# The last norm of a layer taken out of the end and put under the last expert

## The chip, the cores and the metric

The kernel runs on one core of one Trainium2 chip. The metric is the time of one execution on the device in microseconds (us). Engines are named as in the profile: PE (TensorE), DVE (VectorE), ACT (ScalarE), POOL (GpSimd), SP (SyncE); each runs its own instructions in the order in which the kernel writes them down.

## The reference, cut to what matters

One transformer layer: attention and an mLSTM side by side, a norm, a mixture of 16 experts in which each expert picks its 128 tokens of the 1024, and a last norm:

```python
x_new = _layer_norm(ALPHA * x + g1 * mix, ln1_g, ln1_b)
moe = _expert_choice_ffn(x_new * (1 + sc2) + sh2, ...)      # 16 experts, 128 tokens each
x_new = _layer_norm(ALPHA * x_new + g2 * moe, ln2_g, ln2_b) # the norm that is moved
# expert: ((silu(xe @ wg) * (xe @ wu)) @ wd) * g_e, added to the rows idx_e
```

Rows are 1024 wide, an expert's hidden width is 2816. A token can be picked by several experts or by none.

## The kernel before

Only the expert stage and the end matter here. `ACC` is a 1024x1024 table in device memory that holds `ALPHA * x_new`; each expert adds its gated 128 rows to it.

The experts run as 96 steps (`steps`, six for each expert; the last expert is steps 90 to 95; step 95 is half as wide). For each step the weights come as tiles of 1 MB (`we_st`, read by SP into 8 buffers), are split by ACT into a rounded part (`weH`, L1362) and by DVE into the rest (`weL`, L1371). PE multiplies three products for each pair. The loop of L1654 writes down for each `i`, in this order:

- PE: gate product of step i (`ps_gu`), transpose of `hh` of step i-1 (`ps_hT`, L1621); ACT and DVE: `hTH` and `hTL` of step i-1 (L1624, L1625);
- ACT and DVE: the two gate tiles of step i+1; then the piece `extra[2 * i]`, if there is one;
- PE: up product of step i; ACT and DVE: the two up tiles of step i+1;
- PE: down product of step i-1 (`ps_y`, L1635). After an expert's last one DVE gates it into `yo` (L1641) and POOL scatters it with an adding indirect DMA into `ACC` (L1688);
- ACT and DVE: `hh` of step i (L1613, L1614), the two down tiles of step i; then the piece `extra[2 * i + 1]`.

`extra` holds small pieces of work at fixed places; before, only the top-k of the first experts used it. `weH` and `weL` have six buffers each, so a tile is split at most about one step ahead of PE.

The end (`load_z`, `finish`): the two rows of norm weights (`lnv2`) and the 1024 rows of `ACC` are read during step 95 (`zt`, L1650). The last expert's rows are not scattered: after its down product DVE gates them (L1641), ACT and DVE split them (L1798, L1799), and PE adds them to each of eight blocks of 128 rows through a 0/1 matrix (`sel`, L1809, L1810). For each block DVE adds and sums (L1811), ACT squares (L1814) and takes the root, DVE scales by the weights (L1816), ACT by the root (L1821), POOL adds the bias (L1822), and SP writes `out_y` (L1823; the last two blocks in halves by DVE, L1827, L1829).

Of the kernel before, what the change touches and what calls it, by code (L numbers as in the profile page):

```python
# [8 lines left out]
F32 = mybir.dt.float32  # L9
F32R = mybir.dt.float32r  # L10
BF16 = mybir.dt.bfloat16
# [150 lines left out]
def f32(ap):  # L162
    return ap.bitcast(F32)


class K:
# [1151 lines left out]
    def phase_tail(self, nexp=NE, final=True):  # L1318
# [309 lines left out]
        def down(i, h, py):  # L1628
            e, s = steps[i]
            n = 4 if s < 5 else 2  # L1630
            for k in range(n):
                H, L = conv[i, "d", k // 2]
                for m, (a, b) in enumerate(((h[0], H), (h[0], L), (h[1], H))):
                    for j in range(2):
                        nc.tensor.matmul(py[j], a[:, k, :], b[:, k % 2, 512 * j:512 * j + 512],  # L1635
                                         start=(s == 0 and k == 0 and m == 0), stop=(s == 5 and k == n - 1 and m == 2))

        def gated(py, g, out):
            for j in range(2):
                cs = slice(512 * j, 512 * j + 512)  # L1640
                nc.vector.scalar_tensor_tensor(out[:, cs], py[j], g, g2[:, cs], op0=ALU.mult, op1=ALU.mult)  # L1641

        zs = []

        def load_z(n):
            if not zs:
                self.lnv2 = [self.brow(rp, f"ln2{j}", d["lnv"][2 + j:3 + j, :], tag=f"R{j}") for j in range(2)]
            while len(zs) < n:
                zt = self.stage.tile([128, 2, D], F32, name="zt", tag="st")
                nc.sync.dma_start(zt, self.ACC[256 * len(zs):256 * len(zs) + 256].rearrange("(a p) c -> p a c", p=128))  # L1650
                zs.append(zt)

        extra = self.topk_pieces(R)
        for i in range(N + 1):  # L1654
            if i < N:
# [4 lines left out]
            if i > 0:  # L1660
                hT = trans(i - 1, hh)
                if i < N and s == (5 if e == 1 else 4) and e + 1 < nexp:
                    info[e + 1] = self.index_of(e + 1, oh, mx, final and e + 2 == nexp)
                if i + 1 < N:
                    conv_to(end[i + 1, "g"])
                if final and i == N - 1:
                    load_z(3)
                if 2 * i in extra:
                    extra[2 * i]()
# [9 lines left out]
            if i > 0:  # L1679
                ep, sp = steps[i - 1]  # L1680
                if sp == 0:
                    py = [self.pY.tile([128, 512], F32, name="ps_y", tag="y") for _ in range(2)]
                down(i - 1, hT, py)
                if sp == 5 and not (final and i == N):
                    idx, g = info[ep][:2]
                    yo = rp.tile([128, D], F32, name="yo", tag="yo")
                    gated(py, g, yo)
                    nc.gpsimd.indirect_dma_start(out=self.ACC, in_=yo, in_offset=None, compute_op=ALU.add,  # L1688
                                                 out_offset=bass.IndirectOffsetOnAxis(ap=idx[:, :1], axis=0))
            if i < N:  # L1690
                hh = act_mul(i, pg, pu)
# [5 lines left out]
        if final:  # L1697
            load_z(4)
            self.finish(gated, py, info[nexp - 1], zs, mx, mA)
        es.close()  # L1700
# [44 lines left out]

    def index_of(self, e, oh, mx, last=False):
        nc, rp = self.nc, self.rp
# [15 lines left out]
        nc.gpsimd.tensor_add(g, ax[:, 5:6], ax[:, 4:5])  # L1763
        if last:
            nc.gpsimd.tensor_scalar(ax[:, 6:7], ax[:, 0:1], 128.0, ax[:, 1:2], op0=ALU.mult, op1=ALU.add)
            nc.gpsimd.tensor_scalar(ax[:, 8:16], self.tid[:, 1:9], -128.0, ax[:, 6:7], op0=ALU.mult, op1=ALU.add)
        return idx, g, xe, ax
# [14 lines left out]

    def finish(self, gated, py, info, zs, mx, pool):

        nc, d, rp = self.nc, self.d, self.rp
        idx, g, xe, ax = info
        lg, lb = self.lnv2
        sel = mx.tile([128, 8, 128], F32R, name="sel", tag="xe")
        for c in range(8):
            nc.vector.tensor_scalar(sel[:, c, :], self.slots, ax[:, 8 + c:9 + c], None, op0=ALU.is_equal)  # L1790
        yo = rp.tile([128, D], F32, name="yo", tag="yo")
        yH = mx.tile([128, D], F32R, name="yH", tag="xeH")
        yL = mx.tile([128, D], F32R, name="yL", tag="xeL")
        gated(py, g, yo)
        nc.scalar.activation(rp.tile([128, 1], F32, name="tiny"), self.eps, AF.Sqrt)
        for i in range(2):
            cs = slice(512 * i, 512 * i + 512)
            nc.scalar.copy(yH[:, cs], yo[:, cs])  # L1798
            nc.vector.tensor_sub(yL[:, cs], yo[:, cs], f32(yH[:, cs]))  # L1799
        s = rp.tile([128, 8, 8], F32, name="fst")  # L1800
        junk = rp.tile([128, D], BF16, name="junk", tag="oh")
        zt = [zs[t // 2][:, t % 2, :] for t in range(8)]
        wt = [pool.tile([128, D], F32, name="fw", tag=("weH", "weL")[t % 2]) for t in range(8)]

        def add(t):
            for i in range(2):
                cs = slice(512 * i, 512 * i + 512)
                ps = self.pG.tile([128, 512], F32, name="ps_z", tag="g")
                nc.tensor.matmul(ps, sel[:, t, :], yH[:, cs], start=True, stop=False)  # L1809
                nc.tensor.matmul(ps, sel[:, t, :], yL[:, cs], start=False, stop=True)  # L1810
                nc.vector.scalar_tensor_tensor(zt[t][:, cs], ps, 1.0, zt[t][:, cs], op0=ALU.mult, op1=ALU.add,  # L1811
                                               accum_out=s[:, t, i:i + 1])
            nc.vector.tensor_scalar(s[:, t, 2:3], s[:, t, 0:1], s[:, t, 1:2], -1.0 / D, op0=ALU.add, op1=ALU.mult)
            nc.scalar.activation(junk, zt[t], AF.Square, bias=s[:, t, 2:3], accum_out=s[:, t, 3:4])  # L1814
            nc.scalar.activation(s[:, t, 4:5], s[:, t, 3:4], AF.Sqrt, scale=1.0 / D, bias=self.eps)
            nc.vector.scalar_tensor_tensor(wt[t], zt[t], s[:, t, 2:3], lg, op0=ALU.add, op1=ALU.mult)  # L1816

        def scale(t):
            nc.vector.reciprocal(s[:, t, 4:5], s[:, t, 4:5])
            if t < 6:  # L1820
                nc.scalar.activation(wt[t], wt[t], AF.Copy, scale=s[:, t, 4:5])  # L1821
                nc.gpsimd.tensor_add(wt[t], wt[t], lb)  # L1822
                nc.sync.dma_start(self.o["y"][128 * t:128 * t + 128], wt[t])  # L1823
                return
            for i in range(2):
                cs = slice(512 * i, 512 * i + 512)
                nc.vector.scalar_tensor_tensor(wt[t][:, cs], wt[t][:, cs], s[:, t, 4:5], lb[:, cs], op0=ALU.mult,  # L1827
                                               op1=ALU.add)
                nc.sync.dma_start(self.o["y"][128 * t:128 * t + 128, cs], wt[t][:, cs])  # L1829

        for t in range(8):
            add(t)
            if t:
                scale(t - 1)
        scale(7)


# [29 lines left out]
```

## Time and profile before

| | us |
|---|---|
| median of 3 runs (lowest to highest) | 2413.16 (2404.59 to 2416.39) |
| profiled execution | 2414.1 |
| its span in the trace | 2412.3 |
| PE busy in the span | 2253.0 (93%) |
| DVE busy | 1986.7 (82%) |
| ACT busy | 1443.7 (60%) |
| POOL busy | 553.4 (23%) |

The span runs from the first to the last instruction. "Busy" is an average over the whole span; the expert stage takes about its last two thirds, the end about 43 us. A row of the timeline gives the start, the time from the first start to the last end of a run of like instructions, engine, line and operation; in brackets stands how long the engine was idle before it and what ended that.

### The profile page before, as it was taken

The page shows a single profiled execution, that of the slowest core. Times are in us where ns is not written, and L with a number is a line of the kernel's source. Part 1 is how long each engine was busy: PE and PEld are TensorE (multiplying, and loading weights), DVE is VectorE, ACT ScalarE, POOL GpSimd, SP SyncE. Part 2 cuts the span into 40 slices and gives each one's busy share as a digit, 9 for nine tenths or more (in the row PEclk, how much of TensorE's full clock was granted, in tenths as well). Part 3 has the DMA queues.
Part 4 walks back from the last instruction along what each step waited for, and adds up shares of the span by engine and source line. Part 5 has one row for each costly group of instructions (what it writes and reads, how often), then busy time and mean ns, then how long its engine had stood idle before and what let it go on. Part 6 is the DMA issues. An engine that isn't in the chain of part 4 may idle for free.

```text
span 2412.3 us, 33490 instructions
## 1 busy us (share of the span) xinstructions
PE 2253.0 (93%) x12606; PEld 1934.8 (80%) x12606; DVE 1986.7 (82%) x2379; ACT 1443.7 (60%) x1573; POOL 553.4 (23%) x495
## 2 busy tenths in 40 slices
PE   8978999888999599799999999999999999999994
PEld 7878988778888477588888888888888888888883
DVE  7756587757765699988988989889889889889897
ACT  2333433346754466466776777767767767767774
POOL 3424455414444345520000010000000100100102
PEclk9999999999999699899999999999999999999997
DMA  7576447489967598889999999999999999999992
GB/s 287 202 258 221 132 142 221 145 257 297 278 193 244 201 326 316 305 287 394 373 372 398 371 378 390 372 381 383 371 394 377 369 394 376 372 398 371 380 390 99
DMA packets 357971, 748.93 MB, mean 310 GB/s; under 512 B 17073, under 2 KB 106609, under 8 KB 356145
## 3 DMA queue, kind: packets, MB, share of 16 engines
q1 hardware_dynamic: 345344, 703.99, 80.7%
q0 software_dynamic: 12320, 42.28, 5.9%
q8 instruction: 99, 1.62, 0.3%
q14 instruction: 64, 0.52, 0.1%
q10 hardware_dynamic: 144, 0.52, 0.1%
HBM read 690.35 MB, written 63.72 MB: 313 GB/s over the span
## 4 chain that ended last, share of the span: by engine, by line
PE 69%; DVE 15%; DMA 8%; issue 4%; ACT 3%; SPq 1%; POOL 0%; DVEq 0%; ACTq 0%; POOLq 0%
PE ps_gu L1606 36%; PE ps_y L1635 18%; DVE weL L1371 3%; PE ps_o L1408 3%; DMA wr<-in_w_ada 2%; DMA abi<-in_bias 2%; PE ps_in L438 2%; PE ps_hT L1621 1%; PE ps_o L1145 1%; DVE y L546 1%; ACT weH L1362 1%; DVE wr L643 1%; PE ps_in L325 1%; PE ps_xe L1777 1%; DVE m L1722 1%
## 5 line engine op out<-in xcount | busy, mean ns | idle before, releaser
L1371 DVE TENSOR_TENSOR weL<-we_st,weH 128x2048 fp32r<-128x2048 f32 x512 | 1172.7, 2337 | 84.7 <-ACT weH L1362 84.7
L1362 ACT CAST weH<-we_st 128x2048 fp32r<-128x2048 f32 x528 | 982.4, 1915 | 55.7 <-PE ps_y L1635 38.7
L1606 PE MATMUL ps_gu<-weH,xeH 128*128 128x512 f32 (+1 forms) x1536 | 582.5, 379 | 0.0
L1606 PE MATMUL ps_gu<-weL,xeH 128*128 128x512 f32 (+1 forms) x1536 | 573.6, 373 | 1.0 <-DVE weL L1371 1.0
L1606 PE MATMUL ps_gu<-weH,xeL 128*128 128x512 f32 (+1 forms) x1536 | 573.8, 374 | 0.0
L1606 PEld LDWEIGHTS ps_gu<-weH,xeL 128*128 128x128 f32 x1536 | 290.7, 189 | 51.9 <-DVE xeL L1780 0.3
L1606 PEld LDWEIGHTS ps_gu<-weL,xeH 128*128 128x128 f32 x1536 | 291.4, 190 | 50.4 <-DVE weL L1371 1.4
L1606 PEld LDWEIGHTS ps_gu<-weH,xeH 128*128 128x128 f32 x1536 | 291.1, 190 | 48.9 <-ACT xeH L1779 0.2
L1624 ACT CAST hTH<-ps_hT 128x512 fp32r<-128x512 f32 x96 | 52.9, 552 | 411.2 <-PE ps_hT L1621 411.2
L1635 PE MATMUL ps_y<-weH,hTH 128*128 128x512 f32 x704 | 219.3, 393 | 0.5 <-ACT hTH L1624 0.5
L1635 PE MATMUL ps_y<-weH,hTL 128*128 128x512 f32 x704 | 217.7, 391 | 0.5 <-DVE hTL L1625 0.3
L1635 PE MATMUL ps_y<-weL,hTH 128*128 128x512 f32 x704 | 217.8, 391 | 0.0
L1759 POOL TENSOR_SCALAR idx<-ax 128x1 int32<-128x1 f32 x15 | 6.6, 442 | 668.4 <-ACT ax L1752 668.4
L1635 PEld LDWEIGHTS ps_y<-weH,hTL 128*128 128x128 f32 x704 | 132.5, 188 | 29.2 <-DVE hTL L1625 1.3
L1635 PEld LDWEIGHTS ps_y<-weL,hTH 128*128 128x128 f32 x704 | 132.7, 189 | 27.9
L1635 PEld LDWEIGHTS ps_y<-weH,hTH 128*128 128x128 f32 x704 | 131.5, 189 | 27.1 <-ACT hTH L1624 0.7
L438 PE MATMUL ps_in<-wH,uH 128*128 128x256 f32 (+1 forms) x448 | 134.1, 299 | 12.6 <-DVE ev L485 8.7
L1688 POOL DMA_INDIRECT ACC<-yo,idx x15 | 24.2, 1614 | 487.0 <-DVE yo L1641 487.0
L438 PE MATMUL ps_in<-wL,uH 128*128 128x256 f32 (+1 forms) x448 | 131.3, 293 | 0.0
L438 PE MATMUL ps_in<-wH,uL 128*128 128x256 f32 (+1 forms) x448 | 131.1, 293 | 0.0
L1371 POOL TENSOR_TENSOR weL<-we_st,weH 128x2048 fp32r<-128x2048 f32 x16 | 97.4, 6090 | 113.5 <-ACT weH L1362 109.6
L1625 DVE TENSOR_TENSOR hTL<-ps_hT,hTH 128x512 fp32r<-128x512 f32 x96 | 61.6, 642 | 70.1 <-ACT hTH L1624 70.1
(396 smaller groups left out, 3817.0 us busy)
## 6 DMA issues: line engine op xcount, KB each, us to landing
we_st<-in_wg SPq DMA_DIRECT2D x176, 1024.0 KB, 10.0
we_st<-in_wu SPq DMA_DIRECT2D x176, 1024.0 KB, 10.1
we_st<-in_wd SPq DMA_DIRECT2D x176, 1024.0 KB, 9.7
wr<-in_w_ada SPq DMA_DIRECT2D x32, 512.0 KB, 4.4
ws<-in_w_in POOLq DMA_DIRECT2D x36, 256.0 KB, 3.7
abi<-in_bias SPq DMA_DIRECT2D x16, 480.0 KB, 7.3
wa<-in_w_ada SPq DMA_DIRECT2D x7, 1024.0 KB, 7.5
avr<-AVC SPq DMA_DIRECT2D x32, 192.0 KB, 4.6
```

What stands on the lines that cost most here:

```text
L325: nc.tensor.matmul(ps[:, :w], a[:, k, ms], b[:, k, t0:t0 + w], start=(k == 0 and i == 0), stop=(k == 7 and i == 2))
L438: nc.tensor.matmul(ps[:, :w], l, r, start=(k == 0 and i == 0), stop=(k == 7 and i == 2))
L546: nc.vector.scalar_tensor_tensor(y[:, o:o + w], x[:, i0 + j:i0 + j + w], cw[:, j:j + 1], y[:, o:o + w], op0=ALU.mult, op1=ALU.add)
L643: nc.vector.tensor_tensor_reduce(w, w, scr, 1.0, 0.0, ALU.mult, ALU.add, self.ada_r[:, n:n + 1])
L1362: nc.scalar.copy(H, staged[pos[2]])
L1371: (eng or (nc.gpsimd if pool else nc.vector)).tensor_sub(L, staged.pop(pos[1]), f32(H))
L1408: nc.tensor.matmul(ps, a[:, k, :], b, start=(k == 4 and j == 0), stop=(k == 3 and j == 2))
L1606: nc.tensor.matmul(ps[:, :w], a[:, k, :], b[:, kk, :], start=(n == 0), stop=(n == 23))
L1624: nc.scalar.copy(hH[:, :n], pt[:, :n])
L1625: nc.vector.tensor_sub(hL[:, :n], pt[:, :n], f32(hH[:, :n]))
L1635: nc.tensor.matmul(py[j], a[:, k, :], b[:, k % 2, 512 * j:512 * j + 512], start=(s == 0 and k == 0 and m == 0), stop=(s == 5 and k == n - ...
L1688: nc.gpsimd.indirect_dma_start(out=self.ACC, in_=yo, in_offset=None, compute_op=ALU.add, out_offset=bass.IndirectOffsetOnAxis(ap=idx[:, :1 ...
```

## The change

No product with a 0/1 matrix and no `finish` over all rows any more. A class `NormAhead` puts pieces into `extra` from step 88 on. All eight blocks t of `ACC` are normed without the last expert's share and written to the output. The last expert's own 128 rows are gathered from `ACC`, get the share added at the end, are normed and written over the others with an indirect DMA. The order of the last down product changes too (`down_last`: all of its first half of columns, then the second).

`at` is 180, and in the plan `stats` is `stats_v`, `a` is `scale_a`, `b` is `scale_b`. The pieces stand at these places (181 is the end of i = 90, 182 the middle of i = 91, and so on to 192, the middle of i = 96):

```diff
+        at = 2 * first
+        pieces[at - 4] = self.consts
+        take, stats, a, b = self.take, self.stats_v, self.scale_a, self.scale_b
+        plan = {1: (take, 0, 1), 2: (stats, 0), 3: (a, 0, stats, 1), 4: (b, 0), 5: (a, 1, take, 2), 6: (b, 1),
+                7: (stats, 2, take, 3, self.stage, 2, 3), 8: (a, 2, stats, 3), 9: (b, 2, a, 3, self.stats_s, 4),
+                10: (b, 3, a, 4, self.rows, 0), 11: (b, 4, a, 5, self.stats_s, 6), 12: (b, 5, a, 6, 7, b, 6)}
...
+    def buf(self, i):
+        if i % 2:
+            return self.k.rp.tile([128, D], F32, name="zy", tag="yo")
+        return self.mx.tile([128, D], F32, name="zx", tag="xe", bufs=1)
+
+    def rows(self, i):
+
+        self.own = self.buf(i)
+        idx = self.idx
+        self.nc.gpsimd.indirect_dma_start(out=self.own, out_offset=None, in_=self.k.ACC,
+                                          in_offset=bass.IndirectOffsetOnAxis(ap=idx[:, :1], axis=0))
+
+    def take(self, t):
+        z = self.zt[t] = self.buf(t)
+        self.nc.gpsimd.dma_start(z, self.k.ACC[128 * t:128 * t + 128])
+
+    def stage(self, i):
+        z = self.k.stage.tile([128, 2, D], F32, name="zt", tag="st")
+        self.nc.sync.dma_start(z, self.k.ACC[256 * i:256 * i + 256].rearrange("(a p) c -> p a c", p=128))
...
+    def stats_v(self, t):
+        nc, s = self.nc, self.s[:, t]
         for i in range(2):
...
+            nc.vector.bn_stats(s[:, 6 * i:6 * i + 6], self.zt[t][:, 512 * i:512 * i + 512])
+        nc.vector.bn_aggr(s[:, 12:14], s[:, 0:12])
+        self.root(s)
+
+    def root(self, s):
+
+        nc = self.nc
+        nc.gpsimd.tensor_add(s[:, 14:15], s[:, 13:14], self.k.eps)
+        nc.gpsimd.tensor_tensor(s[:, 15:16], s[:, 14:15], self.k.mhalf, op=ALU.pow)
+        nc.gpsimd.tensor_scalar(s[:, 16:17], s[:, 12:13], s[:, 15:16], -1.0, op0=ALU.mult, op1=ALU.mult)
+
+    def stats_s(self, t):
...
+        two = [(self.s[:, i], self.zt[i]) for i in (t, t + 1)]
+        for s, z in two:
+            nc.scalar.activation(junk, z, AF.Identity, accum_out=s[:, 0:1])
+            nc.gpsimd.tensor_scalar(s[:, 1:2], s[:, 0:1], -1.0 / D, None, op0=ALU.mult)
+            nc.gpsimd.tensor_scalar(s[:, 12:13], s[:, 0:1], 1.0 / D, None, op0=ALU.mult)
+        for s, z in two:
+            nc.scalar.activation(junk, z, AF.Square, bias=s[:, 1:2], accum_out=s[:, 2:3])
+            nc.gpsimd.tensor_scalar(s[:, 13:14], s[:, 2:3], 1.0 / D, None, op0=ALU.mult)
+            self.root(s)
+
+    def scale_a(self, t):
+        s, z = self.s[:, t], self.zt[t]
+        self.nc.scalar.activation(z, z, AF.Identity, scale=s[:, 15:16], bias=s[:, 16:17])
+
+    def scale_b(self, t):
+        nc, z = self.nc, self.zt[t]
+        nc.vector.tensor_mul(z, z, self.lg)
+        nc.vector.tensor_add(z, z, self.lb)
+        (nc.gpsimd if t < 4 else nc.sync).dma_start(self.k.o["y"][128 * t:128 * t + 128], z)
+
+    def finish(self, py, info, g2):
...
+        z = self.buf(1)
+        halves = [slice(512 * i, 512 * i + 512) for i in range(2)]
+        for i, cs in enumerate(halves):
+            nc.vector.scalar_tensor_tensor(z[:, cs], py[i], g, g2[:, cs], op0=ALU.mult, op1=ALU.mult)
+            nc.vector.tensor_add(z[:, cs], z[:, cs], self.own[:, cs])
+            nc.vector.bn_stats(s[:, 6 * i:6 * i + 6], z[:, cs])
+        nc.vector.bn_aggr(s[:, 12:14], s[:, 0:12])
+        self.root(s)
+        self.scale_b(7)
+        for cs in halves:
+            nc.vector.scalar_tensor_tensor(z[:, cs], z[:, cs], s[:, 12:13], self.lg[:, cs], op0=ALU.subtract,
+                                           op1=ALU.mult)
+        for cs in halves:
+            nc.vector.scalar_tensor_tensor(z[:, cs], z[:, cs], s[:, 15:16], self.lb[:, cs], op0=ALU.mult, op1=ALU.add)
+        nc.gpsimd.indirect_dma_start(out=self.k.o["y"], in_=z, in_offset=None,
+                                     out_offset=bass.IndirectOffsetOnAxis(ap=idx[:, :1], axis=0))
```

Blocks 0 to 3 are read one by one by POOL (`take`) into two buffers that are also `xe` and `yo`; blocks 4 to 7 by SP (`stage`) into two of the weights' buffers.

## Rows read from the trace of the kernel before

**Rows 1.** The windows view, core 0: each stretch of the last expert and of the end with its length, busy time (and instructions) of PE, PE's weight loads, DVE, ACT and POOL, the granted PE clock, the DMA engines' busy share and GB/s.

```profile
2305.00:2320.00 15.00, 15.00 (x69) 12.41 (x69) 14.12 (x9) 10.48 (x8) 0.00 (x0) 1.00 1.04 397
2320.00:2337.00 17.00, 17.00 (x78) 14.06 (x78) 14.79 (x9) 12.03 (x8) 0.00 (x0) 1.00 1.06 388
2337.00:2354.00 17.00, 17.00 (x80) 14.10 (x79) 14.79 (x10) 10.20 (x7) 0.00 (x0) 1.00 1.02 415
2354.00:2370.00 16.00, 14.72 (x89) 12.62 (x87) 7.17 (x15) 4.74 (x7) 0.00 (x0) 1.00 0.15 59
2370.00:2412.00 42.00, 13.14 (x32) 7.29 (x32) 38.53 (x63) 20.09 (x32) 14.15 (x6) 0.60 0.25 100
```

**Rows 2.** The chain of work that ended last, in order of time (start, length, what): the transpose of step 91, the down product of step 94, the last down product, the gate of the result.

```profile
2308.85 0.44 PE ps_hT L1621 x4
...
2360.01 5.47 PE ps_y L1635 x24
...
2366.16 2.80 PE ps_y L1635 x11
...
2368.99 0.76 DVE yo L1641
```

**Rows 3.** The timeline of DVE in the end: the scaling by the norm's weights of the third block, and the last writes of DVE.

```profile
2378.99 3.29 DVE L1816 SCALAR_TENSOR_TENSOR fw<-zt,fst,ln 128x1024 f32<-128x1024 f32 x1
...
2407.78 1.41 DVE L1827 SCALAR_TENSOR_TENSOR fw<-fw,fst,ln 128x512 f32<-128x512 f32 x2
```

**Rows 4.** Groups of instructions by line and shape over the whole span (busy us, mean ns of one, idle before): the nearest forms to those that the change adds, on DVE, ACT and POOL.

```profile
L1416 DVE BATCH_NORM_STATS2 lst<-z 128x6 f32<-128x512 f32 x16 | 11.1, 695 | 0.6
...
L1430 DVE SCALAR_TENSOR_TENSOR h<-h,lst,B 128x1024 f32<-128x1024 f32 x8 | 10.3, 1285 | 0.3
...
L1437 ACT ACTIVATE xt<-z,lst 128x1024 f32<-128x1024 f32 x8 | 9.9, 1236 | 0.5 <-DVE lst L1427 0.5
...
L1814 ACT ACTIVATE junk<-zt,fst 128x1024 bf16<-128x1024 f32 x8 | 9.2, 1149 | 5.3 <-DVE fst L1813 5.3
...
L1814 ACT ACTIVATION_READ_ACCUMULATOR junk<-zt,fst 128x1 f32 x8 | 1.5, 186 | 0.0
...
L922 POOL TENSOR_TENSOR mrs<-mrs,mhalf 128x8 f32<-128x8 f32 x4 | 6.6, 1661 | 0.3
...
L1442 POOL DMA_DIRECT2D ACC<-xt x8 | 4.5, 564 | 2.4 <-POOL xt L1441 2.4
...
L921 POOL TENSOR_TENSOR mrs<-mmv,eps 128x8 f32<-128x8 f32 x4 | 0.8, 196 | 9.7 <-DVE mmv L918 9.7
```

**Rows 5.** The timeline of POOL in the last expert and just before: two small operations of one column, and the issue of the last scatter into `ACC`.

```profile
2251.47 2.38 POOL L1762 TENSOR_TENSOR ax<-ax 128x1 f32<-128x1 f32 x1
...
2256.05 0.26 POOL L1765 TENSOR_SCALAR ax<-ax 128x1 f32<-128x1 f32 x1
...
2291.14 1.62 POOL L1688 DMA_INDIRECT ACC<-yo,idx  x1 [34.47 <-DVE yo L1641]
```

**Rows 6.** The view of line 1688, the scatter into `ACC`, all 15: ns of the issue on POOL (least, median, most), and from issue to landing.

```profile
L1688 POOL DMA_INDIRECT ACC<-yo,idx x15: 1598/1613/1633, 948.7 to 2291.1; - x15
...
DMA to landing us min/median/max: 8.8/9.2/9.9
```

**Rows 7.** The view of line 1760, the gather of an expert's 128 rows of 4 KB by POOL while weights stream, all 16: issue to landing.

```profile
DMA to landing us min/median/max: 4.6/7.0/8.5
```

**Rows 8.** The timeline of DVE in the last expert: the split of the tiles of step 92, `hh` of step 91.

```profile
2296.38 8.88 DVE L1371 TENSOR_TENSOR weL<-we_st,weH 128x2048 fp32r<-128x2048 f32 x4
2305.18 0.68 DVE L1614 TENSOR_TENSOR hh<-hh,ps_gu 128x512 f32<-128x512 f32 x1
```

**Rows 9.** The view of DMA issues (out<-in, queue, operation, count, KB each, median us from issue to landing): weights, `ACC` written by POOL, `ACC` read by SP under the last expert, and the output written in the end.

```profile
we_st<-in_wg SPq DMA_DIRECT2D x176, 1024.0 KB, 10.0
...
ACC<-xt POOLq DMA_DIRECT2D x8, 512.0 KB, 3.3
zt<-ACC SPq DMA_DIRECT2D x4, 1024.0 KB, 12.9
...
out_y<-fw SPq DMA_DIRECT2D x6, 512.0 KB, 2.6
...
out_y<-fw SPq DMA_DIRECT2D x4, 256.0 KB, 2.0
```

**Rows 10.** The timeline of ACT from step 95's weights on: the cast of its gate and up tiles, `hTH` of step 94, `hTH` of step 95.

```profile
2343.42 3.71 ACT L1362 CAST weH<-we_st 128x2048 fp32r<-128x2048 f32 x2
...
2357.17 0.59 ACT L1624 CAST hTH<-ps_hT 128x512 fp32r<-128x512 f32 x1 [5.95 <-PE ps_hT L1621]
...
2365.74 0.37 ACT L1624 CAST hTH<-ps_hT 128x256 fp32r<-128x256 f32 x1 [5.91 <-PE ps_hT L1621]
```

**Rows 11.** The timeline of SP's issues: the gate tile of step 95, and the last four writes of the output.

```profile
2323.48 0.37 SPq L1350 DMA_DIRECT2D we_st<-in_wg  x1
...
2407.04 2.52 SPq L1829 DMA_DIRECT2D out_y<-fw  x4
```

**Rows 12.** The windows view again, columns as in group 1, where PE had stood for some us in the middle of the kernel.

```profile
874.00:878.00 4.00, 2.26 (x10) 1.52 (x9) 4.00 (x2) 0.00 (x0) 0.74 (x1) 1.00 0.16 30
878.00:882.00 4.00, 2.25 (x8) 1.97 (x9) 4.00 (x4) 1.10 (x2) 0.00 (x0) 0.69 0.93 337
882.00:886.00 4.00, 4.00 (x17) 3.28 (x16) 3.96 (x12) 4.00 (x3) 0.00 (x0) 0.88 1.04 383
```

More of the change, by code (lines that the diff above doesn't have):

```diff
@@ L1636, in down, with down_last @@
                                          start=(s == 0 and k == 0 and m == 0), stop=(s == 5 and k == n - 1 and m == 2))
+        def down_last(i, h, py):
+            for j in range(2):
+                for k in range(2):
+                    H, L = conv[i, "d", 0]
+                    for m, (a, b) in enumerate(((h[0], H), (h[0], L), (h[1], H))):
+                        nc.tensor.matmul(py[j], a[:, k, :], b[:, k % 2, 512 * j:512 * j + 512], start=False,
+                                         stop=(k == 1 and m == 2))
         def gated(py, g, out):
@@ L1641, in gated @@
                 nc.vector.scalar_tensor_tensor(out[:, cs], py[j], g, g2[:, cs], op0=ALU.mult, op1=ALU.mult)
[L1643 to L1651, printed above, removed]
         extra = self.topk_pieces(R)
+        ahead = self.norm_ahead(mx, (nexp - 1) * 6, extra) if final else None
         for i in range(N + 1):
@@ L1662, in phase_tail @@
                 if i < N and s == (5 if e == 1 else 4) and e + 1 < nexp:
-                    info[e + 1] = self.index_of(e + 1, oh, mx, final and e + 2 == nexp)
+                    info[e + 1] = self.index_of(e + 1, oh, mx)
                 if i + 1 < N:
                     conv_to(end[i + 1, "g"])
-                if final and i == N - 1:
-                    load_z(3)
                 if 2 * i in extra:
@@ L1682, in phase_tail @@
                     py = [self.pY.tile([128, 512], F32, name="ps_y", tag="y") for _ in range(2)]
-                down(i - 1, hT, py)
+                (down_last if final and i == N else down)(i - 1, hT, py)
                 if sp == 5 and not (final and i == N):
@@ L1689, in phase_tail @@
                                                  out_offset=bass.IndirectOffsetOnAxis(ap=idx[:, :1], axis=0))
+                    if final and ep == nexp - 2:
+                        ahead.idx = info[nexp - 1][0]
             if i < N:
@@ L1697, in phase_tail @@
         if final:
-            load_z(4)
-            self.finish(gated, py, info[nexp - 1], zs, mx, mA)
+            ahead.finish(py, info[nexp - 1], g2)
         es.close()
@@ L1744, in slots_of, with index_of @@
         return oh
-    def index_of(self, e, oh, mx, last=False):
+    def index_of(self, e, oh, mx):
         nc, rp = self.nc, self.rp
@@ L1763, in index_of @@
         nc.gpsimd.tensor_add(g, ax[:, 5:6], ax[:, 4:5])
-        if last:
-            nc.gpsimd.tensor_scalar(ax[:, 6:7], ax[:, 0:1], 128.0, ax[:, 1:2], op0=ALU.mult, op1=ALU.add)
-            nc.gpsimd.tensor_scalar(ax[:, 8:16], self.tid[:, 1:9], -128.0, ax[:, 6:7], op0=ALU.mult, op1=ALU.add)
         return idx, g, xe, ax
@@ L1781, in tokens_of @@
         return xH, xL
[L1783 to L1795, printed above, removed]
-        for i in range(2):
[L1797 to L1835, printed above, removed]
```

23 lines of the change are left out of this document (added).

## The prediction

> **What bounds the kernel now.** I read the windows of the last expert first [rows 1]: PE is busy in all of every stretch up to 2354 and its clock is granted in full, so PE sets the pace. DVE is close behind (14.8 of 17.0). The 42 us from 2370 on are the end, with PE busy 13.1 and DVE 38.5: DVE bounds it. The chain of waits [rows 2] says the same: PE without a break to the last down product, which ends at 2368.97; then DVE's gate at 2368.99 and DVE nearly to the end. In DVE's timeline the reader should see why the end is so long [rows 3]: a scaling over 1024 columns takes 3.29 us, where a like pass alone took 1.28 [rows 4]; in the end POOL adds a bias beside it, for six of the eight blocks.
>
> **What is removed** is all of this from 2368.99 to 2412.3, 43.3 us. **What is added** goes to DVE, ACT, POOL and the queues under the last expert, and a shorter end. The added rows' durations: an `a` 1.1 us of ACT (L1437 1.24, less when the next follows); a pass of `stats_s` 1.27 (L1814 1.15 and its accumulator read); a bn_stats 0.70, with aggregation `stats` 1.5; a `b`, two passes over 1024 columns in a row, 2.5 (L1430 1.285) [rows 4].
>
> DVE's budget alone: it is idle 5.3 us in the three stretches from 2305 to 2354 and 8.8 in the next [rows 1], 14.1 together. Added are 4 `stats` (6.0) and 7 `b` (17.5), 23.5 us. So the last expert can't hide all of it: 9.4 us are over before anything waits. But it does wait, in three places, and so I follow the path.
>
> *1. First read of `ACC`.* `take(0)` reads rows that the last scatter adds to, so POOL must see that landed. The scatter is issued at 2291.14 [rows 5] and lands 9.2 later [rows 6], at 2300.3. The trace of before has no read of that size by POOL under the weights; nearest is the gather of 128 rows by the same queue, 7.0 (4.6 to 8.5) [rows 7], and I take that: 2307.3. DVE comes to `stats(0)` after the second of four splits that began at 2296.38, at 2.2 each at 2300.8 [rows 8]. It stands 6.5 us, and behind it stand the two up tiles and `hh(91)`, for which PE's transpose waits. In before, `hh(91)` ended at 2305.86 and the transpose began at 2308.85 [rows 2, 8]: cover of 3.0 us. With 6.5 and 1.5 more it ends at 2313.9, and PE stands 5 us.
>
> The Trainium skill speaks against this place: "DMA: Bandwidth & Descriptors", section "Two DMAs through the same engine are not ordered", says that a DMA which reads what an earlier one wrote has to be held until the earlier one's completion semaphore, even on the same queue. No row here shows that wait, as before `ACC` was read only from 2337 on. Without it the read would be in at about 2299.8 and the forecast 6.5 us less; that is a rival below.
>
> *2. DVE without a gap.* From 2307.3 DVE is the last everywhere, since PE was set back 5 us and needs its `hh`: until `stats(2)` is done it runs 16 splits (35.2), 5 `hTL` or `hh` (0.68 alone [rows 8], 0.6 in a row, 3.0), 3 `stats` (4.5) and `b(0)`, `b(1)` (5.0), 47.7 us: 2355.0.
>
> *3. `take(3)` behind `root(2)`.* In POOL's order it follows the root of block 2: add 0.2, power (1.66 for 8 columns; for one 0.2 to 1.66, I take 0.4), and 0.3 [rows 4, 5]. Issue at 2355.9; the weights are in by then, so I take 4.0 to landing, between 3.3 for `ACC` written and the gather's 4.6 [rows 7, 9]: 2359.9. DVE has only `hTL(93)` and one split (2.8) before `stats(3)`, so it stands 2.1. `stats(3)` ends at 2361.4; then split, `hh(94)`, two splits, `b(2)`, 9.7: 2371.1.
>
> *4. ACT behind POOL behind DVE.* Piece 189 writes `b(2)` with its DMA on POOL ahead of `stats_s(4)`. ACT's Square of block 4 needs a mean that POOL works out behind that DMA, which waits for `b(2)`; and behind the Squares ACT has `hTH(94)`, for which PE's down product waits. So: 2371.1, issue 0.56, mean 0.26, two Squares 2.5, `hTH` 0.5: 2374.9. That product began at 2360.01 [rows 2]; PE is 14.9 us late, where `hTH(94)` had followed its transpose at once [rows 10].
>
> *5. ACT's own list* up to `hTH(95)`: `a(4)` 1.1, Silu 0.4, cast 1.8, `a(5)` 1.1, four passes 5.1, `hTH` 0.4: 9.9, to 2384.8 (before 2366.1 [rows 10]). PE's product and transpose are done at 2380.5, so ACT is last here.
>
> *6. DVE's list:* `hTL` 0.4, `b(5)`, `b(6)` 5.0: 2390.2. The last down product (2.8 [rows 2]) is done at 2387.6.
>
> *7. The new end:* two halves of gate, add and bn_stats (0.7 each) 4.0; aggregation 0.2; `b(7)` 2.5, beside which the last root runs; two times two half passes at 1.4 [rows 3] 2.8: 9.5, to 2399.7. Then POOL's indirect write: the output's 512 KB by SP take 2.6 in the empty end [rows 9], the gather at least 4.6 [rows 7]; I take 4.0. In before, the last issue on SP is at 2409.2 [rows 11], lands 2.0 later [rows 9], and the span ends 1.1 after that; the same 1.1 here. End of span 2404.8.
>
> That is 7.5 us under the span of 2412.3. The profiled execution took 2414.1, 0.9 more than the median of the runs, 2413.16; 7.5 under that median is 2405.7, my forecast 2405.5. Of the 43.3 us removed, the new end takes 14.6, and 21.2 are lateness at its start (2390.2 against 2369.0).
>
> *At nothing* I cost the removed index arithmetic on POOL, the two weight rows moved to step 88, and the weights' traffic: a tile is issued some 20 us ahead of its cast (2323.48 against 2343.42) [rows 10, 11] and lands in 10.0 [rows 9], while `take(0)` and `take(1)` bring 1 MB, 2.6 us at 388 GB/s [rows 1]. Were this cover gone, those 2.6 us would come on top. Also the clock: after PE had stood 1.7 us in one window and again in the next, it was granted 0.69 and then 0.88 over 4 us each [rows 12], a part of them at the lower of its two levels (1.2 of 2.4 GHz); about 1.7 us of work lost. The same behind the waits of places 1 and 4 is hidden, as DVE and then ACT are the later ones.
>
> *Bounds.* Place 1: scatter 8.8 to 9.9, read 4.6 to 8.5, so -2.8 to +2.2. Place 3: 2.6 to 8.5 for the read, but DVE can win only its 2.1, so -1.4 to +4.5. The power at 1.66 instead of 0.4 counts at the roots of blocks 2 and 6: up to +3. The last write: 2.6 to 9.2 (the scatter under load), -1.4 to +5, likely near the low end in an empty end. Together not all at once: 2399 to 2412.
>
> **The rivals.**
>
> *No stall at the first read* (the read lands before DVE is there): place 1 falls away, 6.5 us, 2399. For it: the gather once took 4.6. Against it: even that leaves 4 us of wait after a scatter that lands in at least 8.8 [rows 6, 7].
>
> *All hidden:* the end begins at 2368.99, then 9.5 and 5.1: 2383.6 in the span, 2384.5. Against it is DVE's budget, 9.4 us over [rows 1].
>
> *Slower, by reads that land late:* SP's reads of `ACC` under the last expert took 12.9 [rows 9]. If `take(0)` and `take(3)` took that too, place 1 would cost 5.9 more and place 3 8.9 more: 2420. It turns slower when both together are 7.5 over my values, as at about 9.3 and 9.2. For it: the same table at the same time. Against it: those were 1 MB each, four in line behind weights on one queue; the gather on POOL's queue took 7.0 beside the same stream [rows 7].
>
> *POOL held up by DVE:* a one-column operation with two inputs took 2.38 us beside DVE's splits, one with a single input 0.26 [rows 5]. Each such wait adds about 2 us, and with three or four of them on the path, at the roots of blocks 2, 4, 6 and at the end, the time is 2411 to 2415. I count such waits only where DVE runs a split or a `b` at that moment, and after `stats(2)`, the Squares and the last aggregation it mostly doesn't. The Trainium skill goes further ("SBUF — State Buffer", section "SBUF: two separate sides"): a DMA issued from POOL can't get its descriptors written while DVE holds the port that the two share, in its two-port modes; three DMAs on the path would then add some 6 us. By that rule this rival would hold; but no row shows such a stop beside these splits: the 15 scatters were issued in 1.598 to 1.633 us each [rows 6].
>
> **How the numbers follow.** The forecast (2399 to 2412) 0.63; no stall 0.12; all hidden 0.05; late reads 0.08; POOL held up 0.12. A difference under 0.5%, 12.1 us, is what a measurement of this kernel can't tell from none; faster is under 2401.1, slower over 2425.2. Faster: 0.11 of the forecast's 0.63, most of no stall, all of all hidden: 0.27. Slower: the upper part of late reads, 0.03. Same: 0.70. The range 2394 to 2415 leaves out all hidden, late reads and some of the ends, under 0.2.
>
> **What would show it.** Right: DVE idle some 6 us ahead of the first bn_stats, released by the `take`; PE idle 4 to 5 us ahead of the transpose of step 91 and over 5 us ahead of the last full down product, released by ACT; ACT idle ahead of the Square of block 4 until POOL; the last gate some 20 us later than before, and about 15 us from it to the end. Wrong: PE whole until the last product (then all hidden), or reads over 9 us (then no gain).

## The result, and the profile after

The changed kernel takes 2435.32 us (median of 6 runs, 2427.88 to 2439.47) against 2411.59 us of the kernel before in as many runs beside it: ratio 1.0095, 95% interval 1.0079 to 1.011. It is slower by 23.7 us, where 7.5 us less were forecast. Its profiled execution took 2438.0 us, its span 2436.2.

The first thing to look at is where it begins to be late. Up to the last scatter all engines have the same instructions in the same order as before, but for two small operations on POOL that fall away and two reads of weight rows that come in, all in expert 14; still that scatter, issued at 2291.14 before [rows 5], is issued at 2317.43. So 26.3 us are lost before any norm of the change runs, and 18.6 of them by the end of expert 9 (table below). From there to the end of the span it is 118.8 us, and 121.2 before (2412.3 - 2291.14): in the part that was changed 2.4 us are gained, as these two profiles have it.

The windows view of the kernel after, columns as in [rows 1]: 200 us in the middle of the experts, then stretches of the last expert and the end.

```profile
1500.00:1700.00 200.00, 200.00 (x957) 165.03 (x956) 177.61 (x120) 141.12 (x101) 14.79 (x10) 1.00 1.00 377
...
2322.00:2337.00 15.00, 13.66 (x60) 10.74 (x58) 7.76 (x8) 9.11 (x6) 2.23 (x3) 1.00 1.04 371
2337.00:2354.00 17.00, 13.10 (x50) 10.77 (x51) 15.45 (x12) 8.67 (x6) 9.11 (x6) 0.80 0.81 293
...
2386.00:2402.00 16.00, 9.94 (x68) 8.85 (x66) 11.19 (x10) 10.04 (x9) 8.14 (x6) 1.00 0.16 52
2402.00:2420.00 18.00, 11.11 (x38) 8.38 (x38) 12.38 (x12) 14.43 (x22) 13.79 (x27) 0.81 0.36 136
2420.00:2436.00 16.00, 0.00 (x0) 0.00 (x0) 9.99 (x14) 0.79 (x1) 3.96 (x4) 0.62 0.27 110
```

The first stretch in the kernel before:

```profile
1500.00:1700.00 200.00, 200.00 (x985) 168.40 (x984) 177.76 (x119) 140.01 (x101) 18.50 (x13) 1.00 1.03 381
```

In the middle PE is busy all the time and its clock is granted in full, as before, and yet it does 957 instructions in 200 us, not 985: each expert takes longer. In the last expert PE stands where the prediction had it, with 1.3 us missing in 15 and 3.9 in the next 17, where its clock falls to 0.80, and with 6.1 and 6.9 around the last full down product. In the end DVE has 10.0 us of work instead of 38.5 [rows 1]. What is longer in the middle is shown by the chain. In the kernel after (start, length, what):

```profile
1740.52 5.60 PE ps_gu L1606 x24
1746.12 0.44 PE ps_hT L1621 x4
1746.56 5.55 PE ps_gu L1606 x24
1752.11 5.52 PE ps_y L1635 x24
1757.63 5.60 PE ps_gu L1606 x24
```

24 products of 512 columns take 5.52 to 5.60 us. In the changed kernel with its tiles at their old addresses (run e1_pad below) the same rows of the chain are:

```profile
1742.41 5.44 PE ps_gu L1606 x24
1747.86 0.44 PE ps_hT L1621 x4
1748.29 5.49 PE ps_gu L1606 x24
1753.78 5.44 PE ps_y L1635 x24
```

From the starts of the matmuls in the traces: one of 512 columns begins 227.3 ns (mean) after the one before it, in the kernel before, throughout; this distance in time is called the pitch below. In the kernel after it is 228.0 with the weights of two of the six buffers and 233.3 with those of the other four.

The change took two small tiles away, `fst` (256 bytes a partition, L1800 of before) and `tiny` (32 with its rounding, L1795). All that is laid out behind them starts 288 bytes lower: the stationary tiles `xe` and `hT` and two of the weight buffers. Four weight buffers hang at the other end of the memory and stay.

```
bytes in a partition     before                     after
xeH / hTH                99840 / 110080             99552 / 109792
weH, two buffers         114176, 122368             113888, 122080
weH, four buffers        146944 ... 171520          146944 ... 171520
```

The matmuls at 228 ns are those whose two tiles both moved, those at 233 the ones whose stationary tile alone moved. At first those of a buffer that moved take longer as well: where its weights come behind those of one that stayed (71 such places), the first five matmuls start 229 to 233 ns after one another, and from the ninth on it is 226.7.

### The profile page after: what moved, and what is told of

Its sections match the earlier page's. It is cut to its first block, busy times and chain, and to the rows that moved or that the text cites. A ratio compares the mean times of both kernels' runs of the same rounds, so it can differ in the third digit from the quotient of the medians.

```text
span 2436.2 us, 33416 instructions
## 1 busy us (share of the span) xinstructions
PE 2274.4 (93%) x12574; PEld 1935.5 (79%) x12574; DVE 1983.2 (81%) x2346; ACT 1444.4 (59%) x1563; POOL 572.2 (23%) x536
## 4 chain that ended last, share of the span: by engine, by line
PE 66%; DVE 16%; DMA 8%; issue 5%; ACT 3%; POOL 1%; SPq 1%; POOLq 0%; DVEq 0%; ACTq 0%
PE ps_gu L1606 34%; PE ps_y L1635 17%; DVE weL L1371 5%; PE ps_o L1408 3%; PE ps_in L438 3%; DMA abi<-in_bias 1%; PE ps_hT L1621 1%; PE ps_o L1145 1%; DMA wr<-in_w_ada 1%; ACT weH L1362 1%; DMA akL<-AK 1%; PE ps_in L325 1%; DVE m L1721 1%; DVE y L546 1%; PE ps_xe L1773 1%
## 5 line engine op out<-in xcount | busy, mean ns | idle before, releaser
L1371 POOL TENSOR_TENSOR weL<-we_st,weH 128x2048 fp32r<-128x2048 f32 x16 | 92.0, 5751 | 122.6 <-ACT weH L1362 118.8
```

The costliest lines, as they stand in the source:

```text
L1371: (eng or (nc.gpsimd if pool else nc.vector)).tensor_sub(L, staged.pop(pos[1]), f32(H))
```

## The experiments

Theory A is that the addresses cost the 26 us, by the place of one operand's tile against the other's; theory C that each operand's own place counts; rival B that it is something else in the new program. For the last expert, theory D is that DVE's work and its stalls set the end, as the prediction's sum has it; rival E that ACT does, which stands behind POOL's root, which stands behind DVE.

### Where the tiles lie: e1 to e5, e11 to e13

**e1_pad.**

```diff
+        k.rp.tile([128, 72], F32, name="padl")
         self.zt = {}
```

> The change with an unused tile of 288 bytes a partition put where the small tiles fst (256 bytes) and tiny (32 bytes) of the kernel before stood, so that every tile behind them starts at the address that it had before the change; no instruction differs from the changed kernel. Theory A (placement): the change freed 288 bytes, everything behind them moved down by 288, four of the six weight buffers did not, and a matmul of 512 columns whose moving and stationary tiles start 32 bytes apart within 64 starts the next one 233.5 instead of 227 ns later. By A the pitch is 227 ns throughout, the last expert begins about 26 us earlier, and the time is 2435.3 - 26.3 = 2409 us (2404 to 2413). Rival B (the program itself: its code, its queues or the DRAM addresses make the unchanged part slow): 2435 us.

2412.19 us, ratio to before 1.0001 (0.9988 to 1.0014); pitch 227.4 ns. B falls. But A's 2409 missed by 3 us: without the addresses the change is worth nothing that a measurement can tell.

**e2_before_moved.**

```diff
-        nc.scalar.activation(rp.tile([128, 1], F32, name="tiny"), self.eps, AF.Sqrt)
+        nc.scalar.activation(self.zeros[:, 64:65], self.eps, AF.Sqrt)
...
-        s = rp.tile([128, 8, 8], F32, name="fst")
+        s = self.zeros[:, :64].rearrange("p (a b) -> p a b", b=8)
```

> The kernel before with nothing of the change: its two small tiles fst and tiny of the last norm lie in the constant tile zeros instead of in tiles of their own, so that all tiles behind them start 288 bytes lower, as in the changed kernel. The same instructions in the same order. Theory A (placement): the pitch of the matmuls is 233.5 ns for the weights of four of the six buffers, and the time is 2411.6 + 26.3 = 2438 us (2432 to 2442), slower than the changed kernel by the 2.4 us that the change gains in the last expert. Rival B (the changed program): 2411.6 us.

2440.82 us, ratio 1.0116 (1.0095 to 1.0138); pitch 233.3 ns with the weights of four buffers. The kernel before, with the same instructions in the same order, is made as slow as the changed one by moving tiles alone (the two intervals overlap). This is what shows that the addresses cost it.

**e3_both_moved.**

```diff
-                es.enter_context(self.pool(name="padr", bufs=1, side="right")).tile([128, 120], F32, name="padr")
+                es.enter_context(self.pool(name="padr", bufs=1, side="right")).tile([128, 192], F32, name="padr")
```

> The changed kernel with the padding tile at the other end of the memory 288 bytes larger: what the change moved stays moved, and the four weight buffers that stood still move down by 288 bytes as well, so that weights and activations start at the same place within 64 bytes again, 32 behind a multiple. Theory A (the two operands' starts against each other): pitch 227 ns throughout, about 2409 us; up to 2416 if some of the loss in the stages before the experts is not mended by it. Theory C (each operand's own start against a multiple of 64 bytes): all weights slow, 2435 + 26 * 2 / 4 = 2448 us. Rival B: 2435 us.

2410.76 us, ratio 1.0 (0.9984 to 1.0017); pitch 227.1. All operands of the experts' matmuls lie 32 bytes off a multiple of 64, and it is as fast as before: theory C falls. What counts is one tile's place against the other's.

**e4_pad32.** As e1, with `[128, 8]`.

> The changed kernel with an unused tile of 32 bytes at the place of the 288: everything behind it starts 256 bytes lower than in the kernel before, and the two operands of a matmul start at the same place within 256 bytes, but not within 512. Theory A, as put with a period of 64 bytes (or 128, or 256): pitch 227 ns throughout, 2409 us. If the period is 512 bytes, or if what counts is that the buffers stand at the old addresses: 233 ns for two thirds of the matmuls, 2435 us.

Pitch 227.3 ns throughout; 2418.39 us in one run, among the runs of before beside it (2403.9 to 2423.05). A distance of 256 bytes costs nothing.

**e5_offsets.**

```diff
-                H = pool.tile([128, kt, w], F32R, name="weH", tag="weH")
-                L = pool.tile([128, kt, w], F32R, name="weL", tag="weL")
+                H = pool.tile([128, 2052], F32R, name="weH", tag="weH")[:, :2048].rearrange("p (k w) -> p k w", k=kt)
+                L = pool.tile([128, 2052], F32R, name="weL", tag="weL")[:, 4:2052].rearrange("p (k w) -> p k w", k=kt)
```

> The kernel before with its twelve weight buffers at different offsets: each is 32 bytes longer, so that the weH buffers start 0 and 32 bytes behind a multiple of 64 in turn, and the weL tiles lie 16 bytes behind the start of their buffers, at 16 and 48. The stationary tiles stay at multiples of 64. Nothing else differs. It measures the matmul's pitch against the distance of the moving tile's start from the stationary one's: theory A says 227 ns at 0 and 233.5 ns at 32; at 16 and 48 it says nothing yet. If only the half of the 64 bytes counts, 16 is like 0 and 48 like 32, half of the matmuls are slow, and the time is about 2411.6 + 22 * (1/2) / (2/3) = 2428 us; if any distance costs, three quarters are slow, about 2436 us.

2439.46 us in one run; within 256 bytes the `weH` tiles lie 0, 32, 128, 160, 192 and 224 behind the stationary ones, the `weL` tiles 16, 48, 80 and 112. The pitch is 231 to 234 ns with every buffer, also with the one whose `weH` lies right (232.4), its `weL` being off by 80. This agreed with no reading of A that counts in 64 bytes, and led to e11 to e13.

**e11_stationary16.**

```diff
-        xH = mx.tile([128, 8, 128], F32R, name="xeH")
+        xH = mx.tile([128, 1040], F32R, name="xeH")[:, 4:1028].rearrange("p (k w) -> p k w", k=8)
```

The same is done to `xeL`, `hTH` and `hTL`.

> The kernel before with all stationary tiles of the experts (xe and hT, high and low parts) 16 bytes behind a multiple of 64, and all weight tiles at multiples of 64, so that every matmul of the experts has the same distance of 16. It tells what e5 left open, where neighbouring matmuls differed. If any distance within 64 bytes costs as 32 does: pitch 233.5 ns for all, 2411.6 + 22 * 3 / 2 = 2445 us. If 16 costs nothing: 227 ns, 2412 us.

2440.26 us in one run, pitch 233.4 ns over all. The stationary tiles lie 16, 80, 144 and 208 bytes off the weights within 256, and each of these is slow (231.8 to 234.8).

**e12_distance64 and e13_distance128.** As e1, with `[128, 24]` and `[128, 40]`.

> The changed kernel with an unused tile of 96 bytes: what e4 had 256 bytes off the other operand is now 192 bytes off it, 64 within 128. If the starts count within 64 bytes: pitch 227 ns throughout, 2410 us. If they count within 128 or 256: 233.5 ns for two thirds of the matmuls, 2434 us.

> The changed kernel with an unused tile of 160 bytes: everything behind it starts 128 bytes lower than in the kernel before, so that the activations and two of the weight buffers lie 128 bytes off the other four within 256. A distance of 256 cost nothing, one of 64 as much as 32. If the starts count within 128 bytes: pitch 227 ns throughout, no lateness that grows from expert to expert, about 2412 us. If they count within 256: 233.5 ns for two thirds of the matmuls, some 1.6 us an expert, about 2435 us.

2436.16 and 2433.91 us, one run each; pitch 233.3 and 232.7 ns with the four buffers, 228 with the two that moved along. Of the distances tried only 0 and 256 keep 227 ns, so what counts is the place within 256 bytes.

The lateness against the kernel before says the same. It is the start of an expert's gate on DVE (first column: the first product of expert 0), minus that of before, in us:

```
                    first   expert 0   4       9       14
after               1.7     6.0        11.4    18.6    26.3
e1_pad              2.4     2.5        2.5     2.5     2.5
e2_before_moved     5.0     6.4        10.7    17.8    25.5
e3_both_moved      -6.2    -6.4       -9.0    -9.5    -9.8
e4_pad32            5.2     4.9        4.7     4.7     4.7
e11_stationary16   -6.5    -2.0        2.7     13.4    24.2
e12_distance64      1.3     5.7        9.7     16.7    24.3
e13_distance128     3.1     4.6        8.4     15.1    22.1
```

In e1 and e6 to e10, which have the same instructions at the same addresses ahead of it, the first column lies between -2.2 and 8.5, so that of a single profile tells nothing. What grows from column to column is the pitch: from expert 4 on about 1.5 us an expert of 94 where four buffers of six are off, and 2.2 where all are (e11). Where none is off, nothing grows: e1 and e4 keep their lateness within 0.5 us, and e3 falls back by 3.6. Worked out for after: 15 experts of some 396 products of 512 columns, two thirds of them 6.0 ns longer, are 24 us; the lateness grows by 24.6.

### The last expert: e6 to e10

All of these stand at the old addresses and are compared by their times and by the stretch from expert 14's gate to the end of the span, which leaves the stages before out: 122.9 us before, 120.5 after, 120.7 in e1_pad.

**e6_stats_later.**

```diff
-   2: (stats, 0), 3: (a, 0, stats, 1), 4: (b, 0), 5: (a, 1, take, 2), 6: (b, 1),
+   3: (stats, 0, 1), 4: (a, 0), 5: (b, 0, a, 1, take, 2), 6: (b, 1),
```

> The changed kernel at the old addresses (as e1_pad), with the statistics of blocks 0 and 1 one place later in the plan (half a step of the last expert), and what follows of blocks 0 and 1 with them; the rest as in the change. In e1_pad DVE stands 6.8 us ahead of the first bn_stats for the read of ACC. Theory D (the sum of the prediction): DVE is the last everywhere behind that stall, so without it the end comes 6.5 us earlier, 2412.2 - 6.5 = 2406 us. Rival E (ACT's list sets the end, because each a stands behind POOL's root, which stands behind DVE's splits): the stall was cover for that, and the time stays within 2 us of 2412.

2404.65 us, ratio 0.9959 (0.9943 to 0.9976); the stretch is 114.5 us, 6.2 less than in e1_pad, whose DVE stood 6.8 there. D holds for this stall: it was on the path with nearly its whole length.

**e7_no_act_pass.**

```diff
-        nc.vector.tensor_mul(z, z, self.lg)
-        nc.vector.tensor_add(z, z, self.lb)
+        nc.vector.scalar_tensor_tensor(z, z, s[:, 12:13], self.lg, op0=ALU.subtract, op1=ALU.mult)
+        nc.vector.scalar_tensor_tensor(z, z, s[:, 15:16], self.lb, op0=ALU.mult, op1=ALU.add)
...
-        nc.gpsimd.tensor_scalar(s[:, 16:17], s[:, 12:13], s[:, 15:16], -1.0, op0=ALU.mult, op1=ALU.mult)
```

The pieces `a` leave the plan.

> The changed kernel at the old addresses, where DVE does the whole scaling of a block in two passes, (z - mean) * gain and then * root + bias, instead of ACT's pass and then two of DVE: ACT has no a any more, POOL one operation less in each root, DVE 7 times some 0.1 us more. The order is that of the change. Rival E (ACT behind POOL's root): the waits of 13.3, 5.6 and 6.2 us that ACT has for POOL in e1_pad are gone and with them the late hTH tiles, 2412.2 - 7 = 2405 us (2402 to 2408). Theory D (DVE's work and its two stalls for reads set everything): no gain, 2413 us.

2412.49 us (nine of the ten runs 2405.1 to 2417.05, one 8880.88), ratio 0.999 (0.9976 to 1.0003); the stretch is 121.0 us. E's gain isn't there. It isn't a clean refutation of E: the waits view of e7 (us in total, times, the longest) shows a wait of ACT for POOL in another place, as the mean of block 4 is worked out behind POOL's writes of the output, which wait for DVE.

```profile
ACT junk L1856 <- POOL zeros L1853: 16.4, 2, 13.5
```

**e8_rearranged.** The plan, with `stats_s` for blocks 2 to 7 (its mean from the first pass, with a scale of 1/D), and the splits on POOL:

```diff
+        plan = {1: (take, 0, 1), 3: (stats, 0, 1), 5: (b, 0, 1, take, 2, 3), 6: (self.stage, 2),
+                7: (self.stage, 3, self.stats_s, 2), 8: (self.stats_s, 4), 9: (b, 2, 3, self.stats_s, 6),
+                10: (b, 4, self.rows, 0), 11: (b, 5), 12: (b, 6)}
...
+                if final and i >= N - 4:
+                    pool = (kind, hh) in ((("g", 1), ("u", 1)) if i < N - 1 else (("u", 0),))
```

> The changed kernel at the old addresses with everything that stood in its last expert moved out of the way: statistics of blocks 0 and 1 one place later (no wait for the scatter on DVE); no ACT pass (as e7); the statistics of blocks 2 to 7 on ACT, whose mean comes from the scale of the first pass and so waits for nothing on POOL; reads of blocks 2 and 3 behind their buffers' writes and ahead of any root; all regular writes of y on SP; and 7 of the weight splits of the last four steps on POOL instead of DVE. By the sum: DVE has 3.4 us for two statistics, 8 times 2.6 for the scaling and 16 us less splits, so 8 us more than before in 80 us in which it had 14 idle; PE runs to its last product at about 2370 to 2374 of the span, the end takes 14.5, and the time is 2388 us (2384 to 2396). If DVE and POOL, working beside each other, hold each other up at the splits: 2400 or more.

2412.72 us, ratio 0.9995 (0.9981 to 1.0009). The last case of the expectation came. The timelines of DVE and of POOL in e8, two splits each at the same time:

```profile
2308.48 12.81 DVE L1373 TENSOR_TENSOR weL<-we_st,weH 128x2048 fp32r<-128x2048 f32 x2 [1.12 <-ACT weH L1362]
```

```profile
2307.76 9.17 POOL L1373 TENSOR_TENSOR weL<-we_st,weH 128x2048 fp32r<-128x2048 f32 x2
```

Two of DVE's splits take 4.49 us elsewhere; here they last as long as POOL's two and their own together. What was taken off DVE came back as time in which DVE was held. The Trainium skill ("SBUF — State Buffer", section "Who interferes with whom") says that a DVE instruction with two SBUF inputs and a GpSimd instruction that reads SBUF shut each other out, and the later one waits for the whole of the earlier. These rows agree: 9.17 + 4.49 = 13.7, and from the start of POOL's first split to the end of DVE's second it is 13.5 us (2307.76 to 2321.29).

**e9_read3_early.** On e6:

```diff
-   6: (b, 1),  7: (stats, 2, take, 3, self.stage, 2, 3)
+   6: (b, 1, take, 3),  7: (stats, 2, self.stage, 2, 3)
```

> As e6_stats_later, and the read of block 3 stands directly behind block 1's scaling in POOL's order, ahead of the root of block 2. In e6 DVE stands 7.0 us for that read ahead of the statistics of block 3. Theory D (DVE's work and its stalls set the end): that wait goes, 2404.7 - 6 = 2399 us (2397 to 2401). Rival: ACT's list of the tail, which waits for POOL's root of block 3, ends the stretch in any case, and the time stays at 2403 to 2405.

2401.32 us, ratio 0.9941 (0.9919 to 0.9963); the stretch is 111.7 us, 2.8 less than e6, not 6. DVE's wait for the read did not go, it only shrank from 7.0 to 4.3 us. The waits view (us in total, times, the longest), of e6 and then of e9:

```profile
DVE zeros L1836 <- DMA zy<-ACC: 7.0, 1, 7.0
```

```profile
DVE zeros L1836 <- DMA zy<-ACC: 4.3, 1, 4.3
```

POOL's timeline in e9 has the reason: the read has to wait 9.0 us until block 1's write of the same buffer has landed.

```profile
2351.59 0.54 POOL L1826 DMA_DIRECT2D zy<-ACC  x1 [9.00 <-DMA out_y<-zy]
```

**e10_best.** e8 without the splits on POOL, and

```diff
+        plan = {1: (take, 0, 1), 3: (stats, 0, 1), 5: (b, 0, 1, take, 2, 3), 7: (self.stage, 2, 3), 8: (self.stats_s, 2),
+                9: (b, 2, self.stats_s, 4), 10: (b, 3, self.rows, 0), 11: (b, 4), 12: (b, 5, self.stats_s, 6, b, 6)}
```

> The changed kernel at the old addresses, arranged as e8 but with all weight splits on DVE again and the reads of blocks 4 to 7 behind the last weight load, blocks 6 and 7 last. By theory D: DVE gets 3.4 us of statistics and 8 scalings of 2.6 us, 24 us, and had 14 idle under the last expert, so the last gate comes some 10 us later than in the kernel before, at 2379 of a span that begins its last expert at 2289.5; with the end of 15.9 us as in e8: 2396 us (2391 to 2402), faster than e9. If waits come back at other places, as ACT's statistics behind their reads: 2402 or more.

2396.86 us (2392.53 to 2407.99) where 2396 was expected, ratio 0.9933 (0.9911 to 0.9955): faster than both kernels, by 18 us than the one before as it ran beside it (2415.03). The stretch is 107.4 us. The last gate comes 91.8 us after expert 14's, 79.5 before: 12.3 late, 10 expected. The windows view of e10 shows where that comes from: DVE is busy in nearly all of the stretches from 2286 to 2334.

```profile
2286.00:2302.00 16.00, 16.00 (x74) 13.25 (x73) 16.00 (x11) 12.82 (x9) 2.81 (x3) 1.00 1.04 370
2302.00:2318.00 16.00, 16.00 (x75) 13.21 (x74) 15.93 (x15) 11.23 (x9) 1.52 (x4) 1.00 1.04 399
2318.00:2334.00 16.00, 15.21 (x69) 12.28 (x68) 15.79 (x11) 11.04 (x8) 0.00 (x0) 1.00 1.05 394
...
2350.00:2366.00 16.00, 12.12 (x70) 10.73 (x69) 11.10 (x8) 15.84 (x21) 5.40 (x10) 0.89 0.26 103
```

## Why the prediction was wrong

**The step that failed** is the one that the sum starts from: "The scatter is issued at 2291.14". That is the kernel before's time. I took it for the changed kernel's because next to no instruction ahead of it changed, and the list of what costs nothing doesn't name the two tiles that the change drops. It was issued 26.3 us later, as the matmuls of 512 columns started 233.3 instead of 227.3 ns apart with the weights of four buffers of six. No rival had it either; the range ended 20 us below the result.

**From the scatter on** the path was the one forecast and some sizes were too small; in two places POOL was held up by DVE where the prediction had no such wait. In us after the scatter's issue:

| | forecast | measured |
|---|---|---|
| `stats(0)` begins (place 1) | 16.2 | 16.9 |
| `stats(2)` done (place 2) | 63.9 | 66.0 |
| `stats(3)` begins (place 3) | 68.8 | 72.8 |
| `b(2)` done | 80.0 | 83.9 |
| last gate (places 4 to 6) | 99.1 | 103.2 |
| end of the span (place 7) | 113.7 | 118.8 |
| the same before | | 121.2 |

The rows of the chain of the kernel after to which this goes back, in order of time: the last gate of expert 14, the scatter, the two reads, their statistics, ACT's Squares, and the end.

```profile
2315.75 1.41 DVE yo L1650 x2
2317.43 8.95 DMA ACC<-yo,idx
2326.44 0.79 issue
2327.23 7.10 DMA zx<-ACC
2334.35 1.30 DVE zeros L1835 x2
...
2346.48 0.56 ACT hTH L1624
2347.04 1.82 ACT weH L1362
...
2381.98 1.21 DVE zeros L1835 x2
2384.44 1.81 POOL zeros L1844
2386.25 4.00 DMA zy<-ACC
2390.27 1.30 DVE zeros L1835 x2
...
2402.61 1.25 ACT junk L1856 x2
...
2420.64 0.75 DVE zy L1876
...
2427.56 2.59 DMA out_y<-zt
2430.75 1.32 POOLq L1915
```

*Place 1* was right: scatter 8.95 of 9.2, read 7.10 of 7.0, DVE idle 7.2 of 6.5; e6 shows that nearly its whole length was on the path. POOL held the read until the scatter had landed, and 0.8 us more; that hold, which the prediction has speaking against this place, is what makes it. The rival that had no stall there is out.

*Place 2* took 49 us of 47.7, and it had a gap: DVE waited 1.5 us at 2347 for ACT's `hTH` and cast, which stood behind `a(0)`. For `a(0)` ACT had waited 13.3 us until POOL was done with the root of block 0 (the first line of the waits view below).

*Place 3* is half of the 4.1 us missed up to the gate. The read's 4.0 was right, but its issue came 2.8 us behind `stats(2)`, not 0.9, as POOL's root was held. The timeline of POOL in the kernel after, the roots of blocks 0, 1 and 2:

```profile
2335.97 2.12 POOL L1842 TENSOR_TENSOR zeros<-zeros,eps 128x1 f32<-128x1 f32 x1 [7.54 <-DVE zeros L1836]
2338.17 2.52 POOL L1843 TENSOR_TENSOR zeros<-zeros,mhalf 128x1 f32<-128x1 f32 x1
2340.81 4.49 POOL L1844 TENSOR_SCALAR zeros<-zeros 128x1 f32<-128x1 f32 x1
2346.77 0.19 POOL L1842 TENSOR_TENSOR zeros<-zeros,eps 128x1 f32<-128x1 f32 x1 [1.47 <-DVE zeros L1836]
2347.04 0.56 POOL L1843 TENSOR_TENSOR zeros<-zeros,mhalf 128x1 f32<-128x1 f32 x1
2347.70 0.26 POOL L1844 TENSOR_SCALAR zeros<-zeros 128x1 f32<-128x1 f32 x1
...
2383.51 0.19 POOL L1842 TENSOR_TENSOR zeros<-zeros,eps 128x1 f32<-128x1 f32 x1 [10.10 <-DVE zeros L1836]
2383.78 0.56 POOL L1843 TENSOR_TENSOR zeros<-zeros,mhalf 128x1 f32<-128x1 f32 x1
2384.44 1.86 POOL L1844 TENSOR_SCALAR zeros<-zeros 128x1 f32<-128x1 f32 x1
```

The same three operations take 1.0 us for block 1 and 9.1 for block 0, beside DVE's splits. So what the rival "POOL held up by DVE" had, with a chance of 0.12, was there: I had let it count only where DVE runs a split or a `b` at that moment, took it that mostly none would behind `stats(2)`, and took operations with a single input as free of it; the longest, 4.49 us, is one of those. It cost the 2 us of place 3 and, as these rows read, by way of ACT the 1.5 of place 2, where the rival had three or four such waits on the path. The stop of POOL's DMA issues that the rival adds wasn't there: beside the splits the issues of `take` and of `b`'s writes took 0.54 to 0.63 us.

*Places 4 to 6* came 0.1 longer than forecast: PE stands 7.6 us ahead of the last full down product, for ACT, and 5.2 ahead of the transpose of step 91, for DVE, as forecast. The waits view of the kernel after:

```profile
ACT zx L1862 <- POOL zeros L1844: 18.6, 2, 13.3
...
PE ps_hT L1621 <- DVE hh L1614: 8.0, 3, 5.2
...
PE ps_y L1635 <- ACT hTH L1624: 7.6, 1, 7.6
...
DVE zeros L1835 <- DMA zx<-ACC: 7.2, 1, 7.2
```

*Place 7*: 15.6 us of 14.6. DVE's part took 9.5 as forecast; POOL issued the last write 0.8 later, it landed in 3.4 of 4.0, and the span ended 1.9 after that, not 1.1.

So 7.5 us forecast, 5.1 of them lost to these sizes, 2.4 left; and 26.3 lost to the addresses, of which 24.6 grow under the experts, with a first column of 1.7 that varies from profile to profile. The 2.4 is seen in the trace alone: e1_pad, with the addresses put right, measures 1.0001.

**What stays open**: why the distance costs. The pitch depends on nothing else that was looked at: in the slow matmuls of after it is 233 ns whether DVE and ACT work beside them or not. Neighbours count as well: in e5 even matmuls whose own two tiles lie right took 232 ns, and in after the first ones behind a slow buffer do. Whether the distance of the early stages' tiles matters too wasn't tried by itself.

## What to carry to other kernels

A change that adds or drops a tile moves all tiles behind it: compare the addresses of the matmuls' operands as well as the instructions, and keep the moving and the stationary tiles at the same place within 256 bytes. When a time comes out wrong, find first where the two traces part; a lateness that grows evenly through unchanged work belongs to none of the changed instructions. Under a nearly full DVE a stall of it costs its whole length, so place what waits where its data has come in already, and don't count on POOL to take over splits beside it.

## What the runs showed of the hardware

- A matmul of 512 columns starts 227 ns after the one before if moving and stationary tiles start at the same place within 256 bytes (before, e1, e3, e4), and 232 to 235 ns after it where the weights start 32, 48, 112, 128, 176, 192 or 240 bytes behind the stationary tile within 256 (after, e11, e12, e13); the granted clock in the middle of the kernel is 1.00 before and after. Matmuls whose own tiles match are slow too among others that don't (e5, 232 ns). In the kernel after this costs 24 us over 15 experts, 1% of the kernel.
- An operation on one column on POOL took 0.19 to 0.57 us with neither a split nor a `b` of DVE beside it and up to 4.49 beside two splits, with one input tile as well as with two.
- Two splits on POOL beside two on DVE (e8): 9.17 us on POOL, 12.81 on DVE, where DVE alone takes 4.49.
